# Moving the weight pieces and the small tiles of a decoder layer to the other end of the SBUF partition

## The chip, the core and the metric

The kernel runs on one core of one Trainium2 chip. The metric is device microseconds (us) of one execution, the median of several runs. Durations of single instructions are given in nanoseconds (ns).

## What is computed

One layer of a hybrid decoder on 256 tokens of width 2048, all in float32. The reference, cut to its skeleton:

```
h = rms_norm(x, pre_mix_g)
rq, rk, rv, rg, dq, dk, dv, su, sv = split(h @ w_in)          # 2048 -> 6400
y = concat(retention(rq, rk, rv, rg),                          # 6 heads x 128
           diff_attention(dq, dk, dv),                         # 6 heads x 128
           spatial_gating(su, sv))                             # 4 groups x 128
x = x + rms_norm(y @ w_out, post_mix_g)                        # 2048 -> 2048
h = rms_norm(x, pre_ffn_g)
f = (silu(h @ w_gate) * (h @ w_up)) @ w_down                   # 2048 -> 5632 -> 2048
out = x + rms_norm(f, post_ffn_g)
```

## The kernel before

All big products go through one helper, `matmul_chunk` (line 94). It takes a chunk of at most 512 output columns (384 for the heads of differential attention) and walks over the contraction dimension in blocks of 128 rows (a K-block). A weight piece is two K-blocks. `split_weights` (line 71) loads it into a tile `raw` by DMA, ScalarE rounds it to `hi` (line 75), and VectorE makes `lo = raw - hi` (line 77). `accumulate` (line 80) then issues three matmuls for each K-block and each of the two blocks of 128 tokens, because the activation is split the same way:

```
nc.tensor.matmul(ps, lhsT=a_hi, rhs=wh, start=first, stop=False)   # L83
nc.tensor.matmul(ps, lhsT=a_lo, rhs=wh, start=False, stop=False)   # L84
nc.tensor.matmul(ps, lhsT=a_hi, rhs=wl, start=False, stop=last)    # L85
```

The activation slice (`lhsT`, 128 x 128) is the stationary operand. It is loaded into the array by a weight load, which the profile shows as an engine of its own, PEld. The weight piece (`rhs`, 128 x 512) is the moving operand, streamed from SBUF. So every matmul of a projection reads two places of SBUF: an activation tile, and a weight piece. The transposes and small attention products are put between chunks by generators that `advance()` steps.

The stages, with the stationary activation of each: the input projection (6 retention heads, 6 differential heads, 2 pairs of gating groups) with `x_hi` and `x_lo`; the output projection with `y_hi` and `y_lo`; gate and up, 11 chunks each, with `x1_hi` and `x1_lo`, which take the place of `x_hi` and `x_lo` in the pool `act` (the profile calls both `x_hi`, `x_lo`); down, 4 chunks of 44 K-blocks, with `h_hi` and `h_lo`.

SBUF is given out by pools, in the order in which they are opened, each one behind the one before. `const` and `act` come first, then `wpool` (the weight pieces), `small` and `ft`, then what is opened and closed later: `ypool` (y), the attention tiles, the tiles `oz` of the output projection, and at last `hpool` (h), which takes the place of `ypool` and what followed it. The built program places the operands of the projections so (bytes from the partition's start; a K-block of an activation is 1024 bytes and a token block 512, so all slices of a tile have the tile's remainder by 512; a weight piece is 4096 bytes a slot and its K-blocks start at multiples of 512 from the tile, so this holds for them too):

| tile | role | start | remainder by 512 |
|---|---|---|---|
| x_hi (x1_hi) | stationary | 17760 | 352 |
| x_lo (x1_lo) | stationary | 34144 | 352 |
| hi, 5 slots | moving | 83296 | 352 |
| lo, 5 slots | moving | 103776 | 352 |
| y_hi | stationary | 129504 | 480 |
| y_lo | stationary | 145888 | 480 |
| h_hi | stationary | 129504 | 480 |
| h_lo | stationary | 174560 | 480 |

The pool `small` takes 1152 bytes, which is 2 x 512 + 128; that is where the 128 bytes between the two remainders come from.

Of the kernel before, what the change touches and what calls it, by code (L numbers as in the profile page):

```python
# [32 lines left out]
def trunk(  # L33
# [24 lines left out]

    const = ctx.enter_context(tc.tile_pool(name="const", bufs=1))
    act = ctx.enter_context(tc.tile_pool(name="act", bufs=1))  # L60
    wpool = ctx.enter_context(tc.tile_pool(name="wpool", bufs=5))
    small = ctx.enter_context(tc.tile_pool(name="small", bufs=2))
    ft = ctx.enter_context(tc.tile_pool(name="ft", bufs=2))
    ps_acc = ctx.enter_context(tc.tile_pool(name="ps_acc", bufs=4, space=bass.MemoryType.PSUM))
    ps_tr = ctx.enter_context(tc.tile_pool(name="ps_tr", bufs=2, space=bass.MemoryType.PSUM))
    ps_mx = ctx.enter_context(tc.tile_pool(name="ps_mx", bufs=2, space=bass.MemoryType.PSUM))
# [1 line left out]
    def acc_tile():  # L68
        return ps_acc.tile([P, 512], F32, tag="acc", name="acc")

    def split_weights(src, kbs, width):
        raw = wpool.tile([P, kbs, width], F32, tag="raw", name="raw", bufs=4)
        nc.sync.dma_start(out=raw, in_=src)
        hi = wpool.tile([P, kbs, width], F32R, tag="hi", name="hi")
        nc.scalar.copy(out=hi, in_=raw)  # L75
        lo = wpool.tile([P, kbs, width], F32R, tag="lo", name="lo")
        nc.vector.tensor_tensor(out=lo, in0=raw, in1=hi.bitcast(F32), op=ALU.subtract)  # L77
        return hi, lo

    def accumulate(ps, ah, al, wh, wl, kb, tb, first, last):  # L80
        a_hi = ah[:, kb, tb * P:(tb + 1) * P]
        a_lo = al[:, kb, tb * P:(tb + 1) * P]
# [3 lines that stand above are left out]
# [3 lines left out]
    def advance():  # L89
        for g in list(pending):  # L90
            if next(g, "end") == "end":
                pending.remove(g)

    def matmul_chunk(src, kbs, width, ah, al, lead=0, fine=0, on_tb=None, hooks=(), held=None):
        """accs[tb] = a[tb] @ w over kbs K-blocks; token block 0 runs `lead` subtiles ahead of block 1."""
        accs = [acc_tile() for _ in range(NT)]
        subs = []
        kb = 0
        while kb < kbs:
            n = 1 if kb < fine else 2  # L100
            subs.append((kb, n))
            kb += n
        held = held or {}
        for i in range(len(subs) + lead):
            for tb in range(NT):
                k = i - lead * tb
                if not 0 <= k < len(subs):
                    continue
                k0, n = subs[k]
                if k not in held:  # L110
                    piece = src[k0 // 2]
                    held[k] = split_weights(piece[:, k0 % 2:k0 % 2 + n], n, width)
                hi, lo = held[k]
                for j in range(n):
                    accumulate(accs[tb][:, :width], ah, al, hi[:, j], lo[:, j], k0 + j, tb,
                               k0 + j == 0, k0 + j == kbs - 1)
                if k == len(subs) - 1 and on_tb is not None:
                    on_tb(tb, accs[tb])
            if i < len(hooks) and hooks[i] is not None:
                hooks[i]()  # L120
            advance()
        return accs
# [6 lines left out]
        nc.gpsimd.tensor_scalar(out=ve, in0=sums, scalar1=scale, scalar2=eps, op0=ALU.mult, op1=ALU.add)  # L129
        nc.gpsimd.tensor_tensor(out=out_t, in0=ve, in1=neg_half[:, :n], op=ALU.pow)  # L130

# [1 line left out]
    neg_half = const.tile([P, 8], F32, tag="neg_half", name="neg_half")  # L133
    nc.gpsimd.memset(neg_half, -0.5)
    warm = const.tile([P, 8], F32, tag="warm", name="warm")
# [9 lines left out]
    x_lo = act.tile([P, KB, T], F32R, tag="a_lo", name="x_lo")  # L145
    x_sb = act.tile([P, NT, D], F32, tag="x", name="x_sb")

    # ================= token mixer =================
    with ExitStack() as mctx:
        ypool = mctx.enter_context(tc.tile_pool(name="ypool", bufs=1))  # L150
        y_hi = ypool.tile([P, KB, T], F32R, tag="y_hi", name="y_hi")
# [36 lines left out]
        def load_x(tb):  # L188
            nc.sync.dma_start(out=x_sb[:, tb], in_=x[tb * P:(tb + 1) * P])
            for c in range(4):  # L190
                sq = hd.tile([P, 512], F32, tag="sq1", name="sq1", bufs=1)
                nc.scalar.activation(out=sq, in_=x_sb[:, tb, c * 512:(c + 1) * 512], func=AF.Square,
                                     accum_out=ss_1[:, tb, c:c + 1])
# [171 lines left out]
        def sgu_pair(p, kb, accs):  # L365
# [46 lines left out]
            for g in range(2):  # L412
                put_y(kb + g, ys[g])

        first = {0: split_weights(w_ret[0, 0][:, 0:1], 1, 512)}
        load_xT(0, 1, hi_on_dve=True)
        load_order = [(1, 1, True), (2, 2), (4, 2), (6, 2), (8, 2), (10, 2), (12, 2), (14, 2)]
        hooks = [lambda a=a: load_xT(*a) for a in load_order]
        accs = matmul_chunk(w_ret[0], KB, 512, x_hi, x_lo, fine=2, hooks=hooks, held=first)
        pending.append(ret_head(0, 0, accs, wait=5))  # L420
        accs = matmul_chunk(w_ret[1], KB, 512, x_hi, x_lo,
                            hooks=[lambda: load_x(0), None, lambda: load_x(1), None, token_stats])
        small_loads()
        pending.append(ret_head(1, 1, accs))
        for h in range(2, NH):
            accs = matmul_chunk(w_ret[h], KB, 512, x_hi, x_lo)
            pending.append(ret_head(h, h, accs))
        for h in range(NH):
            accs = matmul_chunk(w_diff[h], KB, 384, x_hi, x_lo)
            pending.append(diff_head(h, NH + h, accs))  # L430
        load_sgu()
        for p in range(NG // 2):
            accs = matmul_chunk(w_sgu[p], KB, 512, x_hi, x_lo)
            pending.append(sgu_pair(p, 2 * NH + 2 * p, accs))

# [1 line left out]
        accs0 = matmul_chunk(w_out[0], KB, 512, y_hi, y_lo)  # L437
        while pending:
            advance()
# [71 lines left out]
            nc.gpsimd.tensor_scalar(out=hr2, in0=rstd2, scalar1=0.5, scalar2=None, op0=ALU.mult)  # L511
            nc.gpsimd.tensor_tensor(out=hrr, in0=hr2, in1=rstd2, op=ALU.mult)

# [1 line left out]
        def start_residual():  # L515
            pending.append(residual())

# [13 lines left out]

        up0 = matmul_chunk(w_up[0], KB, 512, x1_hi, x1_lo, hooks=[None] * 3 + [finish_gate0])

    # ================= feed forward =================
    hpool = ctx.enter_context(tc.tile_pool(name="hpool", bufs=1))
    h_hi = hpool.tile([P, HB, T], F32R, tag="h_hi", name="h_hi")
    h_lo = hpool.tile([P, HB, T], F32R, tag="h_lo", name="h_lo")
# [17 lines left out]
    for c in range(1, NCH):  # L555
        accs = matmul_chunk(w_gate[c], KB, 512, x1_hi, x1_lo)
        aa = [gate_part(tb, accs[tb]) for tb in range(NT)]
        accs = matmul_chunk(w_up[c], KB, 512, x1_hi, x1_lo)
# [124 lines left out]
```

## Time and profile before

| | |
|---|---|
| time, median of 3 runs | 1153.27 us (1153.09 to 1153.86) |
| span of the profiled execution | 1151.1 us |
| TensorE matmul (PE) busy | 1136.2 us, 99% |
| weight load (PEld) busy | 951.0 us, 83% |
| VectorE (DVE) busy | 636.5 us, 55% |
| ScalarE (ACT) busy | 530.1 us, 46% |
| DMA | 221.34 MB, mean 192 GB/s |
| granted TensorE clock | 0.998 |

The span runs from the first to the last instruction of the program; the profiled execution has no time of its own beside it. The timed runs are 2.0 to 2.8 us longer than this span, 2.2 us at the median. A matmul's recorded duration runs from its start to a modelled end, and the next one starts before that end; how fast TensorE goes is read from start to start.

### The profile page before, as it was taken

The numbers are of one execution on the slowest core, as the hardware profiler recorded it, in microseconds if no ns is written. First come the engines' busy times: TensorE is split into PE (matmuls) and PEld (weight loads), VectorE is DVE, ScalarE is ACT, GpSimd is POOL, SyncE is SP. The second block draws the span as 40 slices with busy tenths as digits, with TensorE's granted clock in tenths as the row PEclk, the third lists the DMA queues.
The fourth block names the chain that finished last, engine by engine and source line by source line (L and its number), as shares of the span: only waits on it lengthen the run. The fifth ranks groups of instructions, "written<-read, shape, count | busy, mean of one in ns | idle before, by whom it ended". The sixth has DMA issues, their size and how long they took to land.

```text
span 1151.1 us, 13889 instructions
## 1 busy us (share of the span) xinstructions
PE 1136.2 (99%) x5266; PEld 951.0 (83%) x5266; DVE 636.5 (55%) x759; ACT 530.1 (46%) x720; POOL 27.1 (2%) x56
## 2 busy tenths in 40 slices
PE   7999999999999999999999999999999999999997
PEld 6888899998878778888888888888888888888885
DVE  6655455656767595555555555554554544444444
ACT  7644445656634464444444444444444434343332
POOL 0000000000100000000000000000000000000000
PEclk9999999999999999999999999999999999999999
DMA  9755555565566447556555555555555655655553
GB/s 348 265 187 191 164 165 175 174 214 175 185 219 220 163 150 234 184 187 197 185 188 194 186 189 193 186 193 189 188 196 185 221 194 186 185 190 192 164 184 110
DMA packets 64468, 221.34 MB, mean 192 GB/s; under 512 B 7168, under 2 KB 9232, under 8 KB 63760
## 3 DMA queue, kind: packets, MB, share of 16 engines
q1 hardware_dynamic: 64368, 220.43, 58.3%
q8 instruction: 41, 0.67, 0.3%
q14 instruction: 27, 0.22, 0.1%
q0 software_dynamic: 32, 0.02, 0.0%
HBM read 218.32 MB, written 2.10 MB: 191 GB/s over the span
## 4 chain that ended last, share of the span: by engine, by line
PE 97%; DVE 1%; issue 1%; DMA 0%; ACT 0%; POOL 0%; DVEq 0%; POOLq 0%
PE acc L83 31%; PE acc L85 31%; PE acc L84 31%; PE h_ps L548 1%; PE qk_ps L220 0%; PE sc L252 0%; DMA cols<-in_cols_dram 0%; PE yt_ps L176 0%; DVE x_lo L479 0%; PE o_ps L229 0%; PE o_ps L228 0%; PE o_ps L227 0%; PE sc L329 0%; PE x_ps L476 0%; DVE fg L589 0%
## 5 line engine op out<-in xcount | busy, mean ns | idle before, releaser
L77 DVE TENSOR_TENSOR lo<-raw,hi 128x1024 fp32r<-128x1024 f32 (+2 forms) x409 | 486.1, 1190 | 462.8 <-ACT hi L75 441.2
L75 ACT CAST hi<-raw 128x1024 fp32r<-128x1024 f32 (+2 forms) x409 | 418.5, 1025 | 553.7 <-PE acc L84 496.2
L83 PE MATMUL acc<-hi,x_hi 128*128 128x512 f32 (+1 forms) x1152 | 444.0, 386 | 6.2 <-DVE x_hi L166 6.2
L84 PE MATMUL acc<-hi,x_lo 128*128 128x512 f32 (+1 forms) x1152 | 438.7, 381 | 0.0
L85 PE MATMUL acc<-lo,x_hi 128*128 128x512 f32 (+1 forms) x1152 | 438.6, 381 | 0.0
L83 PEld LDWEIGHTS acc<-hi,x_hi 128*128 128x128 f32 x1152 | 216.8, 188 | 44.2 <-issue 8.1
L85 PEld LDWEIGHTS acc<-lo,x_hi 128*128 128x128 f32 x1152 | 216.7, 188 | 37.9
L84 PEld LDWEIGHTS acc<-hi,x_lo 128*128 128x128 f32 x1152 | 216.9, 188 | 36.8 <-DVE x_lo L169 0.4
L83 PE MATMUL acc<-hi,h_hi 128*128 128x512 f32 x352 | 139.0, 395 | 0.0
L85 PE MATMUL acc<-lo,h_hi 128*128 128x512 f32 x352 | 138.9, 395 | 0.0
L84 PE MATMUL acc<-hi,h_lo 128*128 128x512 f32 x352 | 138.9, 395 | 0.0
L85 PEld LDWEIGHTS acc<-lo,h_hi 128*128 128x128 f32 x352 | 66.3, 188 | 15.6
L84 PEld LDWEIGHTS acc<-hi,h_lo 128*128 128x128 f32 x352 | 66.3, 188 | 15.4
L83 PEld LDWEIGHTS acc<-hi,h_hi 128*128 128x128 f32 x352 | 66.3, 188 | 15.3
L83 PE MATMUL acc<-hi,y_hi 128*128 128x512 f32 x128 | 50.9, 400 | 0.0
L84 PE MATMUL acc<-hi,y_lo 128*128 128x512 f32 x128 | 50.5, 396 | 0.0
L85 PE MATMUL acc<-lo,y_hi 128*128 128x512 f32 x128 | 50.4, 395 | 0.0
L83 PEld LDWEIGHTS acc<-hi,y_hi 128*128 128x128 f32 x128 | 24.0, 188 | 5.8 <-ACT y_hi L178 0.3
L85 PEld LDWEIGHTS acc<-lo,y_hi 128*128 128x128 f32 x128 | 24.1, 188 | 5.5
L84 PEld LDWEIGHTS acc<-hi,y_lo 128*128 128x128 f32 x128 | 24.1, 188 | 5.4
L585 POOL TENSOR_TENSOR ro_f<-ss_t,neg_half 128x1 f32<-128x1 f32 x2 | 1.1, 548 | 711.0 <-DVE ss_t L583 711.0
L520 ACT ACTIVATE fa<-acc,hr 128x512 f32<-128x512 f32 x22 | 15.0, 685 | 5.7 <-PE acc L85 5.3
(133 smaller groups left out, 423.7 us busy)
## 6 DMA issues: line engine op xcount, KB each, us to landing
raw<-in_w_gate_dram SPq DMA_DIRECT2D x88, 512.0 KB, 3.5
raw<-in_w_up_dram SPq DMA_DIRECT2D x88, 512.0 KB, 3.5
raw<-in_w_down_dram SPq DMA_DIRECT2D x88, 512.0 KB, 3.5
raw<-in_w_ret_dram SPq DMA_DIRECT2D x47, 512.0 KB, 4.5
raw<-in_w_diff_dram SPq DMA_DIRECT2D x48, 384.0 KB, 3.3
raw<-in_w_out_dram SPq DMA_DIRECT2D x32, 512.0 KB, 4.2
raw<-in_w_sgu_dram SPq DMA_DIRECT2D x16, 512.0 KB, 4.4
x_sb<-in_x_dram SPq DMA_DIRECT2D x2, 1024.0 KB, 8.1
```

The costliest lines, as they stand in the source:

```text
L75: nc.scalar.copy(out=hi, in_=raw)
L77: nc.vector.tensor_tensor(out=lo, in0=raw, in1=hi.bitcast(F32), op=ALU.subtract)
L83: nc.tensor.matmul(ps, lhsT=a_hi, rhs=wh, start=first, stop=False)
L84: nc.tensor.matmul(ps, lhsT=a_lo, rhs=wh, start=False, stop=False)
L85: nc.tensor.matmul(ps, lhsT=a_hi, rhs=wl, start=False, stop=last)
L520: nc.scalar.activation(out=a, in_=acc, func=AF.Tanh, scale=hr2[:, tb:tb + 1])
L548: nc.tensor.transpose(out=pt[:, i], in_=aa[tb][:, i * P:(i + 1) * P], identity=ident)
L585: nc.gpsimd.tensor_tensor(out=ro_f[:, tb:tb + 1], in0=ss_t[:, tb:tb + 1], in1=neg_half[:, :1], op=ALU.pow)
```

## The change

The three pools `wpool`, `small` and `ft` are opened on the right side, so they are given out from the far end of the partition downwards. What is opened behind them moves down into the space that they leave. Nothing else changes: the instructions of each engine, their order and the semaphores that they wait for are the same in both built programs, since the lifetimes of all tiles and the order of the pools on the left are the same. The diff, without comment lines that it drops:

```diff
-    wpool = ctx.enter_context(tc.tile_pool(name="wpool", bufs=5))
-    small = ctx.enter_context(tc.tile_pool(name="small", bufs=2))
-    ft = ctx.enter_context(tc.tile_pool(name="ft", bufs=2))
+    wpool = ctx.enter_context(tc.tile_pool(name="wpool", bufs=5, side="right"))
+    small = ctx.enter_context(tc.tile_pool(name="small", bufs=2, side="right"))
+    ft = ctx.enter_context(tc.tile_pool(name="ft", bufs=2, side="right"))
```

The operands of the projections then lie so:

| tile | start before | start after | remainder by 512, before | after |
|---|---|---|---|---|
| x_hi, x_lo | 17760, 34144 | the same | 352 | 352 |
| y_hi, y_lo | 129504, 145888 | 66912, 83296 | 480 | 352 |
| h_hi, h_lo | 129504, 174560 | 66912, 111968 | 480 | 352 |
| hi, lo | 83296, 103776 | 188384, 208864 | 352 | 480 |

Stationary less moving, by 512, is 0 in the x stages and 128 in the y and h stages before; it is 384 (the same as -128) in all stages after.

## Rows read from the trace of the kernel before

**Rows 1.** The page: span, busy time by engine, shares of the chain that ended last.

```profile
span 1151.1 us, 13889 instructions
PE 1136.2 (99%) x5266; PEld 951.0 (83%) x5266; DVE 636.5 (55%) x759; ACT 530.1 (46%) x720; POOL 27.1 (2%) x56
PE 97%; DVE 1%; issue 1%; DMA 0%; ACT 0%; POOL 0%; DVEq 0%; POOLq 0%
```

**Rows 2.** Busy time by engine in four stretches: stages x, y, gate/up, down.

```profile
core 0: us, PE busy (x) PEld busy (x) DVE busy (x) ACT busy (x) POOL busy (x), PEclk, DMA share, GB/s
25.00:50.00 25.00, 25.00 (x112) 20.72 (x111) 13.77 (x19) 16.91 (x31) 2.14 (x3) 1.00 0.87 312
...
345.00:385.00 40.00, 40.00 (x174) 32.41 (x173) 30.40 (x29) 18.46 (x26) 0.00 (x0) 1.00 0.65 211
465.00:501.00 36.00, 36.00 (x161) 29.81 (x160) 18.95 (x18) 15.25 (x16) 0.00 (x0) 1.00 0.59 192
1000.00:1041.00 41.00, 41.00 (x178) 33.26 (x177) 18.85 (x18) 16.96 (x19) 0.00 (x0) 1.00 0.59 184
```

**Rows 3.** Groups by line and shape, whole span; L84 of each stationary operand.

```profile
L84 PE MATMUL acc<-hi,x_lo 128*128 128x512 f32 x960 | 374.5, 390 | 0.0
...
L84 PEld LDWEIGHTS acc<-hi,x_lo 128*128 128x128 f32 x1152 | 216.9, 188 | 36.8 <-DVE x_lo L169 0.4
...
L84 PE MATMUL acc<-hi,h_lo 128*128 128x512 f32 x352 | 138.9, 395 | 0.0
L84 PEld LDWEIGHTS acc<-hi,h_lo 128*128 128x128 f32 x352 | 66.3, 188 | 15.4
...
L84 PE MATMUL acc<-hi,x_lo 128*128 128x384 f32 x192 | 64.2, 334 | 0.0
...
L84 PE MATMUL acc<-hi,y_lo 128*128 128x512 f32 x128 | 50.5, 396 | 0.0
```

**Rows 4.** Timeline, PE, gate/up: first and last of 161 matmuls in a row.

```profile
464.67 0.39 PE L85 MATMUL acc<-lo,x_hi 128*128 128x512 f32 x1
...
500.94 0.39 PE L83 MATMUL acc<-hi,x_hi 128*128 128x512 f32 x1
```

**Rows 5.** Timeline, PE, down: first and last of 178 matmuls in a row.

```profile
999.77 0.39 PE L85 MATMUL acc<-lo,h_hi 128*128 128x512 f32 x1
...
1040.90 0.39 PE L85 MATMUL acc<-lo,h_hi 128*128 128x512 f32 x1
```

**Rows 6.** Timeline, PE, output projection: first and last of 174 in a row.

```profile
344.79 0.40 PE L84 MATMUL acc<-hi,y_lo 128*128 128x512 f32 x1
...
384.98 0.40 PE L83 MATMUL acc<-hi,y_hi 128*128 128x512 f32 x1
```

**Rows 7.** Timeline, PE, differential heads: first and last of 45, 384 columns wide.

```profile
199.82 0.33 PE L83 MATMUL acc<-hi,x_hi 128*128 128x384 f32 x1
...
207.45 0.34 PE L85 MATMUL acc<-lo,x_hi 128*128 128x384 f32 x1
```

**Rows 8.** Timeline, PE, gate/up around the transposes between two chunks.

```profile
502.30 1.03 PE L548 MATMUL h_ps<-ident,fa 128*128 128x128 f32 x8
503.09 0.48 PE L83 MATMUL acc<-hi,x_hi 128*128 128x512 f32 x1
503.41 0.39 PE L84 MATMUL acc<-hi,x_lo 128*128 128x512 f32 x1
...
504.79 0.39 PE L84 MATMUL acc<-hi,x_lo 128*128 128x512 f32 x1
...
506.83 0.39 PE L84 MATMUL acc<-hi,x_lo 128*128 128x512 f32 x1
```

## The prediction

> **What bounds the kernel now.** The page comes first: TensorE is busy 99% of the span, and the chain that ended last is 97% TensorE [rows 1]. DVE and ACT have 45% and more of the span to spare, so a change pays or costs only where it alters the pace of the matmuls. [...] No wait is there to be removed. What is left is the spacing of the matmuls while nobody waits, and there the stages differ, which is the finding this forecast rests on.
>
> The groups by shape hint at it: the same line with the same 128x512 shape has a mean of 390 ns with x as stationary, 395 ns with h and 396 ns with y [rows 3]. These durations have a modelled end, so I took start to start from the timeline. Gate/up: 161 starts, (500.94 - 464.67) / 160 = 226.7 ns [rows 4]. Down: 178 starts, (1040.90 - 999.77) / 177 = 232.4 ns [rows 5]. Output projection: 174 starts, (384.98 - 344.79) / 173 = 232.3 ns [rows 6]. So y and h run 5.7 ns a matmul behind x, at the same clock, shape and moving tiles. Differential heads, 384 columns, stationary x: 45 starts, 7.63 / 44 = 173.4 ns [rows 7]. The 128 columns between 384 and 512 cost 53.3 ns, 0.416 ns a column, so 512 columns need 213.3 ns; x pays 13.4 ns on top at either width, y and h pay 19.0. It is a price per weight load, not per column.
>
> What differs between x and y or h is only where the stationary tile lies: higher up in the partition, and with a remainder by 512 bytes that is 128 larger. The moving tiles are the same for all.
>
> Two rows narrow it down. The weight load takes 188 ns for x and for h alike [rows 3]; the loading does not get longer, the matmul that runs over it does. And h covers 90 KB of the partition, y only the lowest 32 KB of that stretch, yet both run at the same 232.3 to 232.4 ns; a price that grew with distance would show. I therefore read it as two streams of reads, the weight load's and the matmul's, that get in each other's way or not depending on how their addresses stand to each other: 0 by 512 is good, 128 is bad.
>
> After a break x is slow for a moment as well: behind the transposes six spacings take (504.79 - 503.41) / 6 = 230 ns, then nine take (506.83 - 504.79) / 9 = 226.7 [rows 8]. So x finds into the faster rhythm within about six matmuls; the y and h stretches of 173 and 177 spacings do not find it.
>
> **The change, part by part.** No instruction, order or wait changes, and with TensorE as the bound [rows 1] the other engines' accesses at new addresses have 45% of slack to hide any difference; I cost them at nothing. What uncovers this is only a VectorE group that grew by more than that 45%, for which no row speaks. The small tiles and `ft` are read by ACT, DVE and the 11 sets of transposes (88 of them); nothing there either. Three edits remain.
>
> y and h move down to x's remainder, 352. There are 128 x 3 matmuls with y and 352 x 3 with h, on three lines each [rows 3]: 1440. If they reach x's spacing they give 1440 x 5.68 = 8.2 us. Some 12 breaks in these stages (the last gating steps, eight sets of transposes of the second norm, the last h) keep up to six slow ones each, 0.4 us, so 7.8 us. The other bound is nothing.
>
> The moving tiles go from 352 to 480. No row shows a moving weight piece at this remainder, so I bound it by the two spacings that exist: 226.7 and 232.4. For the 960 x 3 = 2880 matmuls of 512 columns with x or x1 the loss is between nothing and 2880 x 5.68 = 16.4 us; up to six behind each of about 40 breaks (four TensorE steps in each retention head, 11 sets of transposes, some of the rest) are slow already, 1.2 us, so 15.2 us. The 192 x 3 = 576 matmuls of 384 columns lie between nothing and 3.3 us; as the price goes by the weight load and not by the column, 3.0 us less breaks.
>
> Which value holds depends on the difference of the two addresses, and that is 384 by 512 in every stage after the change: neither the good 0 nor the bad 128. If the pattern repeats every 256 bytes, 384 is 128 and all stages are slow. If it repeats every 512, 384 is a case of its own, and of the two differences seen one is good and one bad. Nothing in these rows can choose between 256 and 512. I take the slow value: one half for sure and part of the other half.
>
> The sum: y and h stay as they are, 0; x at 512 columns +15.2; x at 384 columns +3.0; in all +18.2 us. Against the profiled span, 1151.1 + 18.2 = 1169.3 us; with the 2.2 us by which the median of the timed runs lies above that span, 1171.5 us.
>
> [...] The trace shows one matmul shape at 226.7 and 232.4 ns with nothing changed but the place of its stationary tile [rows 4, 5]. [...]
>
> **Rivals.**
>
> *The stationary tile's own place decides* (faster). Then the remainder 352 is good in itself, or the lower part of the partition is, and the moving tile's place is indifferent. For it: x, the good case, keeps its place, and y and h get exactly its remainder and come down next to it. Against it: the weight load is no longer in the bad case than in the good one [rows 3], so a place that is bad in itself should show there. It also covers a pattern of 512 bytes in which 384 happens to be good. Time: 1153.3 - 7.8 = 1145.5 us. It decides as soon as the x stages keep 226.7 ns; if then only part of h gains (the upper half of h_lo, say, in a matter of height), the time lies between 1145.5 and 1151.
>
> *Nothing changes* (same). Either placement has no effect and the 5.7 ns come from something else that goes with the stage, or the border between good and bad lies between the end of x_lo (50528) and the new start of y and h (66912), so that y and h stay bad and x good. [...] Against it: the two slow stages have different widths of weights in flight, different evacuations and different neighbours, and share with each other only the place. Time: 1153.3 us.
>
> *All stages slow, but worse than 232.4.* A new difference may be worse than the known bad one. No row prices it; the range's top leaves a little room only.
>
> **How the numbers follow.** Two streams in each other's way at 384: 0.48, time 1171.5, its own range 1167 to 1173.5 (without the breaks' allowance and with all 384-wide matmuls, 16.4 + 3.3 = 19.7 gives 1173.0; without the 384-wide ones at all, 15.2 gives 1168.5). Stationary place alone, or 384 good: 0.40, time 1145.5, its own range 1144.8 to 1151. Nothing changes: 0.10. Worse than known: 0.02. The two big cases have opposite signs and nearly the same chance, so the range must reach over both: 1144.8 to 1173.5. Faster by over 0.2% (2.3 us, about what a measurement of this kernel can tell from no change): 0.40; within it 0.10; slower 0.48 + 0.02 = 0.50.
>
> **What the changed profile would show.** Read start to start in the same five places. Right: gate/up and the input projection at about 232 ns, the 384-wide heads near 179, output projection and down still at 232, weight loads still 188 ns, granted clock 1.00, and DVE and ACT busy times within 1% of before. The first rival: gate/up at 226.7 and also y and h at 226.7. The second: all five as before. What would make the prediction wrong in its base rather than its sign: a spacing that is neither 226.7 nor 232.4, DVE or ACT instructions that change their durations with the place, or an idle gap of TensorE that was not there.

## The result, and the profile after

The change makes the kernel slower: 1169.15 us (1168.86 to 1170.53, 4 runs) against 1153.18 us beside it, a ratio of 1.0142 with a 95% interval of 1.013 to 1.0154. The forecast was 1171.5 us within 1144.8 to 1173.5. Of the executions behind the times below, one of the ten of experiment 3 took 1575.26 us at a granted clock of 0.68 and is left out of its ratio; all others were granted 0.99 or more.

The page first: span, busy time by engine, and the shares of the chain that ended last.

```profile
span 1167.3 us, 13889 instructions
PE 1152.5 (99%) x5266; PEld 954.0 (82%) x5266; DVE 637.0 (55%) x759; ACT 529.0 (45%) x720; POOL 26.9 (2%) x56
PE 98%; issue 1%; DMA 0%; DVE 0%; ACT 0%; DVEq 0%; POOL 0%; POOLq 0%
```

The same counts of instructions as in [rows 1], TensorE busy for 16.3 us more, the span 16.2 us longer, the weight loads (PEld) 3.0 us more, and VectorE, ScalarE and GpSimd within 1.1 us of before. No new wait: the time went into TensorE's own busy time. The stretches by window (PE, PEld, DVE, ACT, POOL; clock, DMA share, GB/s), which answer to [rows 2], say the same: no gap, and a granted clock of 1.00.

```profile
350.00:390.00 40.00, 40.00 (x174) 32.43 (x173) 30.14 (x28) 18.42 (x26) 0.00 (x0) 1.00 0.64 209
472.00:508.00 36.00, 36.00 (x157) 29.18 (x156) 18.38 (x18) 14.92 (x15) 0.00 (x0) 1.00 0.58 185
1000.00:1041.00 41.00, 41.00 (x178) 33.26 (x177) 19.13 (x17) 16.94 (x19) 0.00 (x0) 1.00 0.57 188
```

Gate/up has 157 matmuls in 36 us where it had 161; the output projection and down have the same 174 and 178 as before. Start to start in the timeline, first and last row of each stretch (157, 174, 178 and 47 matmuls in a row):

```profile
471.61 0.39 PE L84 MATMUL acc<-hi,x_lo 128*128 128x512 f32 x1
...
507.86 0.39 PE L84 MATMUL acc<-hi,x_lo 128*128 128x512 f32 x1
...
349.64 0.39 PE L85 MATMUL acc<-lo,y_hi 128*128 128x512 f32 x1
...
389.84 0.40 PE L84 MATMUL acc<-hi,y_lo 128*128 128x512 f32 x1
...
999.73 0.39 PE L84 MATMUL acc<-hi,h_lo 128*128 128x512 f32 x1
...
1040.86 0.39 PE L84 MATMUL acc<-hi,h_lo 128*128 128x512 f32 x1
...
202.63 0.34 PE L84 MATMUL acc<-hi,x_lo 128*128 128x384 f32 x1
...
210.72 0.34 PE L85 MATMUL acc<-lo,x_hi 128*128 128x384 f32 x1
```

| stretch | before | after |
|---|---|---|
| gate/up, stationary x1 | 226.7 ns [rows 4] | 36.25 / 156 = 232.4 ns |
| output projection, y | 232.3 ns [rows 6] | 40.20 / 173 = 232.4 ns |
| down, h | 232.4 ns [rows 5] | 41.13 / 177 = 232.4 ns |
| differential heads, x, 384 columns | 173.4 ns [rows 7] | 8.09 / 46 = 175.9 ns |

All stages of 512 columns now have one spacing, the slow one. The mean weight load is as long as it was within 1 ns [rows 3], here for the stationary x and h:

```profile
L84 PEld LDWEIGHTS acc<-hi,x_lo 128*128 128x128 f32 x1152 | 217.5, 189 | 41.1 <-DVE x_lo L169 0.4
...
L84 PEld LDWEIGHTS acc<-hi,h_lo 128*128 128x128 f32 x352 | 66.3, 188 | 15.4
```

The mean hides something. The shortest, median and longest load of one line in gate/up, before and after:

```profile
L84 PEld LDWEIGHTS acc<-hi,x_lo x54: 187/188/188, 464.9 to 500.9; 128*128 128x128 f32 x54
...
L84 PEld LDWEIGHTS acc<-hi,x_lo x52: 187/188/192, 472.1 to 507.6; 128*128 128x128 f32 x52
```

In the fast stretch no load is longer than 188 ns; in the slow one some take 192. In the down stage of the kernel before, slow as well, one load in seven does (152 of 1056), and it is the load that runs in the longest spacing of each seven, 240 or 241 ns. So the loads of a slow stage show it too, by 4 ns in every seventh.

And behind the transposes between two chunks x no longer finds into a faster rhythm, as it did in [rows 8]: thirteen spacings take (513.16 - 510.14) / 13 = 232.3 ns.

```profile
509.03 1.04 PE L548 MATMUL h_ps<-ident,fa 128*128 128x128 f32 x8
509.82 0.48 PE L83 MATMUL acc<-hi,x_hi 128*128 128x512 f32 x1
510.14 0.39 PE L84 MATMUL acc<-hi,x_lo 128*128 128x512 f32 x1
...
513.16 0.39 PE L85 MATMUL acc<-lo,x_hi 128*128 128x512 f32 x1
```

Where the 16.2 us arise is read from landmarks of the program in both timelines and chains. Before:

```profile
149.01 0.33 PE L83 MATMUL acc<-hi,x_hi 128*128 128x384 f32 x1
263.64 0.39 PE L83 MATMUL acc<-hi,x_hi 128*128 128x512 f32 x1
458.05 0.87 PE h_ps L548 x8
902.39 0.87 PE h_ps L548 x8
```

After:

```profile
151.67 0.35 PE L83 MATMUL acc<-hi,x_hi 128*128 128x384 f32 x1
267.57 0.39 PE L83 MATMUL acc<-hi,x_hi 128*128 128x512 f32 x1
463.70 0.87 PE h_ps L548 x8
918.62 0.87 PE h_ps L548 x8
```

The differential heads start 2.7 us later and end 3.9 us later; the first set of transposes of the feed forward comes 5.65 us later, the eleventh 16.23 us; the rest, down with h alone, adds nothing. So the stages of 384 columns cost 1.3 us, the x and x1 stages of 512 columns 16.2 - 1.3 = 14.9 us, y and h nothing.

### The profile page after: what moved, and what is told of

It reads as the page before. It is cut to its first block, busy times and chain, and to the rows that moved or that the text cites. A ratio compares the mean times of both kernels' runs of the same rounds, so it can differ in the third digit from the quotient of the medians.

```text
span 1167.3 us, 13889 instructions
## 1 busy us (share of the span) xinstructions
PE 1152.5 (99%) x5266; PEld 954.0 (82%) x5266; DVE 637.0 (55%) x759; ACT 529.0 (45%) x720; POOL 26.9 (2%) x56
## 4 chain that ended last, share of the span: by engine, by line
PE 98%; issue 1%; DMA 0%; DVE 0%; ACT 0%; DVEq 0%; POOL 0%; POOLq 0%
PE acc L83 32%; PE acc L85 31%; PE acc L84 31%; PE h_ps L548 1%; PE qk_ps L220 0%; PE sc L252 0%; DMA cols<-in_cols_dram 0%; PE x_ps L476 0%; PE yt_ps L176 0%; PE o_ps L229 0%; PE o_ps L228 0%; PE o_ps L227 0%; PE sc L329 0%; DVE fg L589 0%; PE pm L406 0%
## 5 line engine op out<-in xcount | busy, mean ns | idle before, releaser
L83 PE MATMUL acc<-hi,x_hi 128*128 128x512 f32 (+1 forms) x1152 | 449.4, 390 | 6.1 <-DVE x_hi L166 6.1
L84 PE MATMUL acc<-hi,x_lo 128*128 128x512 f32 (+1 forms) x1152 | 444.3, 386 | 0.0
L85 PE MATMUL acc<-lo,x_hi 128*128 128x512 f32 (+1 forms) x1152 | 444.0, 386 | 0.0
L83 PEld LDWEIGHTS acc<-hi,x_hi 128*128 128x128 f32 x1152 | 217.4, 189 | 48.6 <-issue 8.1
L85 PEld LDWEIGHTS acc<-lo,x_hi 128*128 128x128 f32 x1152 | 217.3, 189 | 42.3
L84 PEld LDWEIGHTS acc<-hi,x_lo 128*128 128x128 f32 x1152 | 217.5, 189 | 41.1 <-DVE x_lo L169 0.4
L83 PE MATMUL acc<-hi,h_hi 128*128 128x512 f32 x352 | 139.0, 395 | 0.0
L85 PE MATMUL acc<-lo,h_hi 128*128 128x512 f32 x352 | 138.9, 395 | 0.0
L84 PE MATMUL acc<-hi,h_lo 128*128 128x512 f32 x352 | 138.9, 395 | 0.0
L83 PEld LDWEIGHTS acc<-hi,h_hi 128*128 128x128 f32 x352 | 66.3, 188 | 15.5
L84 PEld LDWEIGHTS acc<-hi,h_lo 128*128 128x128 f32 x352 | 66.3, 188 | 15.4
L85 PEld LDWEIGHTS acc<-lo,h_hi 128*128 128x128 f32 x352 | 66.3, 188 | 15.4
L83 PE MATMUL acc<-hi,y_hi 128*128 128x512 f32 x128 | 50.9, 400 | 0.0
L84 PE MATMUL acc<-hi,y_lo 128*128 128x512 f32 x128 | 50.5, 396 | 0.0
L85 PE MATMUL acc<-lo,y_hi 128*128 128x512 f32 x128 | 50.4, 395 | 0.0
L83 PEld LDWEIGHTS acc<-hi,y_hi 128*128 128x128 f32 x128 | 24.0, 188 | 5.8 <-ACT y_hi L178 0.3
L85 PEld LDWEIGHTS acc<-lo,y_hi 128*128 128x128 f32 x128 | 24.1, 188 | 5.5
L84 PEld LDWEIGHTS acc<-hi,y_lo 128*128 128x128 f32 x128 | 24.1, 188 | 5.4
```

## The experiments

The theory: the difference of the two addresses that TensorE reads at a time, the stationary tile that is being loaded and the moving tile that streams, sets the spacing. (In gate/up of the kernel before, the load for L84 starts at 464.90 us and takes 0.19 us; the matmul of L83 starts at 464.90 us as well, and that of L84 at 465.12 us.) The rivals: the place of the stationary tile, the place of the moving tile (each by its height or by its own remainder). Unused bytes move tiles without changing any instruction.

**1. y and h alone moved by 384 bytes, in the kernel before.**

```diff
     ft = ctx.enter_context(tc.tile_pool(name="ft", bufs=2))
+    gap = ctx.enter_context(tc.tile_pool(name="gap", bufs=1))
+    gap.tile([P, 96], F32, tag="gap", name="gap")
```

> The kernel before with 384 unused bytes behind the pool ft: y and h stay in the upper part of the partition but get the remainder 352 by 512, so stationary less moving is 0 in every stage. If the difference of the two addresses decides: y and h run at 226.7 ns like x, 1145.5 us (ratio to before 0.993). If the height in the partition decides (low is good): nothing changes, 1153 us.

Measured: 1144.96 us, ratio to before 0.993 (0.9916 to 0.9945). Down, first and last of 182 matmuls in a row (the two lines more shift L83 to L85):

```profile
999.80 0.39 PE L85 MATMUL acc<-hi,h_hi 128*128 128x512 f32 x1
...
1040.83 0.39 PE L86 MATMUL acc<-hi,h_lo 128*128 128x512 f32 x1
```

41.03 / 181 = 226.7 ns. y and h lie as high as before, 384 bytes higher in fact, and run like x. Height is out; so is the time of the stage, its width or its neighbours.

**2. The changed kernel with its weight pieces moved by 128 bytes.**

```diff
+    gap = ctx.enter_context(tc.tile_pool(name="gap", bufs=1, side="right"))
+    gap.tile([P, 32], F32, tag="gap", name="gap")
     wpool = ctx.enter_context(tc.tile_pool(name="wpool", bufs=5, side="right"))
```

> The changed kernel with 128 unused bytes at the far end, so the weight pieces lie at the far end with remainder 352 and stationary less moving is 0 everywhere. If the difference decides: all stages at 226.7 ns, 1145.5 us, the same as the kernel before with the unused bytes, and 24 us faster than the changed kernel. If weight pieces at the far end are slow by their place: all stages at 232.4 ns, 1169 us.

Measured: 1145.04 us, ratio 0.993 (0.9914 to 0.9947). With the whole change in place and 128 bytes more, the kernel is 24 us faster than the changed one. The far end is not slow. Gate/up, first and last of 125:

```profile
471.72 0.39 PE L87 MATMUL acc<-lo,x_hi 128*128 128x512 f32 x1
...
499.82 0.39 PE L85 MATMUL acc<-hi,x_hi 128*128 128x512 f32 x1
```

28.10 / 124 = 226.6 ns, where the changed kernel has 232.4.

**3. Everything moved by 128 bytes, in the kernel before.**

```diff
+    gap = ctx.enter_context(tc.tile_pool(name="gap", bufs=1))
+    gap.tile([P, 32], F32, tag="gap", name="gap")
     const = ctx.enter_context(tc.tile_pool(name="const", bufs=1))
```

> The kernel before with 128 unused bytes ahead of every pool: all operands move up by 128 bytes, so every remainder changes (x and weights 480, y and h 96) and no difference does. If the difference decides: as before, x at 226.7 and y and h at 232.4 ns, 1153 us. If the stationary tile's own remainder decides (480 is bad): x goes to 232.4 ns, 1168 us or more; if the moving tile's own remainder decides (480 is bad): all stages at 232.4 ns, 1169 us.

Measured: 1152.78 us, ratio 0.9999 (0.999 to 1.0009), its span 1151.0 us as before. x and the weight pieces now have the remainder 480, which y and h had in the slow case, and x stays at 226.6 ns; y and h have 96, a new one, and stay slow:

```profile
471.83 0.39 PE L86 MATMUL acc<-hi,x_lo 128*128 128x512 f32 x1
...
499.93 0.39 PE L87 MATMUL acc<-lo,x_hi 128*128 128x512 f32 x1
...
999.67 0.39 PE L87 MATMUL acc<-lo,h_hi 128*128 128x512 f32 x1
...
1040.80 0.39 PE L87 MATMUL acc<-lo,h_hi 128*128 128x512 f32 x1
```

(125 and 178 matmuls: 28.10 / 124 = 226.6 and 41.13 / 177 = 232.4 ns.) No tile's own remainder decides. These three leave the difference.

**4. A ladder of differences.** The weight piece of each chunk of gate and up is written a given number of bytes into a wider slot:

```diff
...
+    def piece_tile(kbs, width, tag):
+        t = wpool.tile([P, 1152], F32R, tag=tag, name=tag, bufs=4)
+        o = shift[0] // 4
+        return t[:, o:o + kbs * width].rearrange("p (k w) -> p k w", k=kbs)
...
-        hi = wpool.tile([P, kbs, width], F32R, tag="hi", name="hi")
+        hi = piece_tile(kbs, width, "hi")
...
-        lo = wpool.tile([P, kbs, width], F32R, tag="lo", name="lo")
+        lo = piece_tile(kbs, width, "lo")
...
+        shift[0] = SHIFTS[2 * c]
         accs = matmul_chunk(w_gate[c], KB, 512, x1_hi, x1_lo)
...
```

> A ladder: the kernel before with four slots for hi and lo instead of five, 512 bytes wider each, and in each of the 22 chunks of gate and up the weight piece written that many bytes into its slot: 0, 16, 32 and so on to 192, then in steps of 32 to 288, then 320 to 480. Stationary less moving is minus that many bytes. If the pattern repeats every 256 bytes: 226.7 ns at 0 and 256, 232.4 at 128 and 384, and the second half of the ladder repeats the first. If it repeats every 512 and 384 is bad by itself: the two halves differ. If only whole 128-byte blocks count, the spacing changes at the steps where a block's border is passed and not in between. No other effect on the time than through these spacings is expected; the total lies between 1150 and 1165 us.

**5. The ladder again with fine steps.** Only the list of bytes differs from the first ladder.

> The ladder again with fine steps around the two good places: the 22 chunks of gate and up are written 0, 4, 8, 12, 20, 24, 28, 240, 244, 248, 252, 256, 260, 264, 268, 272, 508, 504, 500, 496, 192 and 0 bytes into their slots. If the pattern repeats every 256 bytes down to its detail: 4 and 260 alike, 8 and 264, 252 and 508, 248 and 504, each pair within 0.3 ns. If the good case is one exact place: only 0 and 256 at 226.7 ns. If it is a window: its neighbours within a few bytes on one or both sides are at 226.7 too.

Measured in both, from the timeline: mean start to start in the later 70 or so matmuls of each chunk, without spacings across a missing record, in ns; another choice of stretch moves a value by about 0.1. The row 0 is the last chunk of the fine ladder, since the first chunk of both lies among breaks. The left column is moving less stationary, by 256; the column "upper" holds the same plus 256. In this count the change puts every stage at 128, and y and h before it stand at 384.

| by 256 | in the lower 256 | in the upper 256 |
|---|---|---|
| 0 | 226.7 | 226.7 |
| 4 | 236.7 | 236.5 |
| 8 | 233.3 | 233.3 |
| 12 | 228.9 | 228.9 |
| 16 | 231.7 | 231.7 |
| 28 | 226.8 | - |
| 32 | 233.2 | 233.3 |
| 64 | 229.0 | 229.0 |
| 96 | 233.4 | 233.3 |
| 128 | 232.4 | 233.3 |
| 160 | 234.1 | 234.3 |
| 192 | 233.3 | 233.3 |
| 224 | 233.3 | 233.3 |
| 240 | 236.7 | 236.7 |
| 244 | 239.8 | 239.9 |
| 248 | 230.0 | 233.3 |
| 252 | 226.7 | 226.7 |

Not in the table: 20 gives 236.0 and 24, 48, 144 and 176 give 233.3; 80 and 112 give 231.1. Two chunks of the fine ladder, at 4 (82 matmuls) and at 256 bytes (92), by first and last row:

```profile
437.81 0.40 PE L92 MATMUL acc<-hi,x_lo 128*128 128x512 f32 x1
...
456.98 0.40 PE L92 MATMUL acc<-hi,x_lo 128*128 128x512 f32 x1
...
663.32 0.39 PE L91 MATMUL acc<-hi,x_hi 128*128 128x512 f32 x1
...
683.95 0.39 PE L92 MATMUL acc<-hi,x_lo 128*128 128x512 f32 x1
```

19.17 / 81 = 236.7 and 20.63 / 91 = 226.7 ns. The pattern repeats every 256 bytes: of 16 pairs 14 agree within 0.3 ns, 128 and 384 are 0.9 ns apart and 248 and 504 are 3.3 apart. A difference can have more than one rhythm: y and h of the kernel before run at 232.4 ns with the difference at which the ladder has 233.3. That settles what the prediction left open: within 1 ns the change's 384 is the known bad 128. The good case is neither one place nor a window: 0, 252 and 28 have it, 4 bytes beside 0 costs 10 ns, and whole 128-byte blocks do not count, since the spacing moves within 4 bytes. The ladders' times were 1168.85 and 1169.53 us (one run each); the first lies above the 1150 to 1165 expected, and the spacings alone do not explain it. By the timeline its span exceeds that of the kernel before by 16.1 us: 11.3 us are the spacings in gate and up (a mean of 232.2 against 226.8 ns), 3.4 us are longer breaks there, nearly all in the first chunk, and 1.2 us arise in down, with ten short breaks that the kernel before lacks. So the expectation that nothing else would act on the time was wrong. TensorE now waits, for the transposes' input and for a weight piece:

```profile
PE x_ps L484 <- DVE hx L480: 1.7, 1, 1.7
PE acc L93 <- DVE lo L85: 1.1, 1, 1.1
```

The ladders have four slots for hi and lo where the kernel before has five, a likely cause that no run tests by itself. The means in the table leave the breaks out.

**6. All operands at multiples of 512.** The kernel of experiment 1 with 160 unused bytes ahead of every pool:

```diff
+    low = ctx.enter_context(tc.tile_pool(name="low", bufs=1))
+    low.tile([P, 40], F32, tag="low", name="low")
     const = ctx.enter_context(tc.tile_pool(name="const", bufs=1))
```

> The first padded kernel (difference 0 in every stage) with 160 more unused bytes ahead of every pool, so that all operands of the projections start at a multiple of 512 bytes. If only the difference counts: the same as that kernel, 226.7 ns in every stage, 1145 us. If the 13.4 ns that even the good case pays on top of its 512 columns come from tiles that start inside a 128-byte block: down to some 213 to 216 ns a matmul, 512 columns alone at the rate of the rows, about 1085 us.

Measured: 1145.48 us, ratio 0.9937 (0.9922 to 0.9952). Down, first and last of 182:

```profile
999.75 0.39 PE L89 MATMUL acc<-lo,h_hi 128*128 128x512 f32 x1
...
1040.78 0.39 PE L87 MATMUL acc<-hi,h_hi 128*128 128x512 f32 x1
```

41.03 / 181 = 226.7 ns again. The 13.4 ns that remain in the good case, by the prediction's estimate from [rows 4, 7], do not come from where tiles start within 512 bytes.

**7. y and h alone put right, in the changed kernel.**

```diff
     ft = ctx.enter_context(tc.tile_pool(name="ft", bufs=2, side="right"))
+    gap = ctx.enter_context(tc.tile_pool(name="gap", bufs=1))
...
     x_sb = act.tile([P, NT, D], F32, tag="x", name="x_sb")
+    gap.tile([P, 32], F32, tag="gap", name="gap")
```

> The changed kernel with 128 unused bytes between x and y: y and h stay low and the weight pieces at the far end, but y and h get the weight pieces' remainder, so their difference is 0 while that of x stays at 384. If the differences act by stage and add up: y and h at 226.7 ns, x at 232.4, the changed kernel's 1169 us less 7.8 us, 1161 us. If what x does disturbs the later stages or the height decides: 1169 us.

Measured: 1161.47 us, ratio to before 1.0077 (1.006 to 1.0094). Gate/up (122 matmuls) and down (183):

```profile
471.65 0.39 PE L84 MATMUL acc<-hi,x_hi 128*128 128x512 f32 x1
...
499.77 0.40 PE L85 MATMUL acc<-hi,x_lo 128*128 128x512 f32 x1
...
999.73 0.39 PE L84 MATMUL acc<-hi,h_hi 128*128 128x512 f32 x1
...
1040.99 0.39 PE L86 MATMUL acc<-lo,h_hi 128*128 128x512 f32 x1
```

28.12 / 121 = 232.4 and 41.26 / 182 = 226.7 ns: the stages are independent and add up, 1169.15 - 7.8 = 1161.35 expected.

**8. Only x_lo at difference 128.** In the kernel before:

```diff
+    act.tile([P, 32], F32, tag="gap1", name="gap1")
     x_lo = act.tile([P, KB, T], F32R, tag="a_lo", name="x_lo")
     x_sb = act.tile([P, NT, D], F32, tag="x", name="x_sb")
+    act.tile([P, 96], F32, tag="gap2", name="gap2")
```

> The kernel before with 128 unused bytes between x_hi and x_lo (and 384 more behind x, so that the weight pieces, y and h keep their remainders): of the three matmuls of a K-block in the x stages only L84's stationary tile lies at difference 128, the other two at 0. L84's weight load runs while the matmul of L83 streams. If the load that runs meanwhile is what gets in the matmul's way: the spacing behind L83 grows and the other two stay near 226.7 ns. If a matmul is slow because of its own stationary tile: the spacing behind L84 grows instead. If any bad load throws the rhythm of all: all three near 232 ns. Time: 1/3 of the whole loss to all of it, 1158 to 1169 us.

Measured: 1165.13 us (one run), inside the range but with none of the three pictures. Three K-blocks in a row from the timeline:

```profile
480.19 0.40 PE L83 MATMUL acc<-hi,x_hi 128*128 128x512 f32 x1
480.42 0.40 PE L84 MATMUL acc<-hi,x_lo 128*128 128x512 f32 x1
480.65 0.39 PE L85 MATMUL acc<-lo,x_hi 128*128 128x512 f32 x1
480.88 0.40 PE L83 MATMUL acc<-hi,x_hi 128*128 128x512 f32 x1
...
482.27 0.40 PE L83 MATMUL acc<-hi,x_hi 128*128 128x512 f32 x1
```

Nine spacings take 2.08 us, 231.1 ns each; over all of gate/up the mean is 232.5 behind L83, 234.1 behind L84 and 226.9 behind L85. The spacing behind the matmul over which the bad load runs (L83) grows, and so does the one behind the next (L84); the third is near the fast value. So my picture that only the matmul streaming meanwhile pays was too simple. The weight loads in gate/up, 465 to 501 us, do not point at the bad tile either (shortest, median, longest):

```profile
L84 PEld LDWEIGHTS acc<-hi,x_lo x53: 187/188/188, 464.9 to 501.0; 128*128 128x128 f32 x53
...
L85 PEld LDWEIGHTS acc<-lo,x_hi x52: 192/192/193, 465.2 to 500.5; 128*128 128x128 f32 x52
```

The load of x_lo, at the bad difference, takes its 188 ns; the one after it, of x_hi at difference 0, takes 192 every time. Whether the second stretch comes from the slow matmul's own tile or is the first one's disturbance carried over stays open.

## Why the prediction was right

*What bounds the kernel.* Right: TensorE stays the bound, busy for 99% of the span, with no gap and a granted clock of 1.00 in the three windows, and the busy times of VectorE and ScalarE stay within 0.2%.

*The difference of the addresses, not the place.* Right, and shown: experiments 1 and 2 put the difference right at either end of the partition and get 226.7 ns everywhere, and experiment 3 moves every place and leaves every difference and gets no change of time. The mechanism behind it, two streams of reads in each other's way, was only argued; the runs show the dependence on the difference, not the collisions. The step "the loading does not get longer" rested on a mean: in the slow stretches of 512 columns about every seventh load takes 192 instead of 188 ns.

*384 is like 128.* The prediction took the slow value, half because a pattern of 256 bytes would force it. It could not choose between 256 and 512 from its rows; the ladder did. So the sign was in good part luck: slower had 0.50 and faster 0.40, and the range had to reach over both.

*y and h stay as they are, 0.* Right: 232.4 ns in both stages.

*x at 512 columns, +15.2 us.* Measured 14.9. (At the 5.68 ns and six matmuls a break that gave 0.4 us for 12 breaks, 40 breaks come to 1.4 us and not 1.2, and the term to 15.0.)

*x at 384 columns, +3.0 us.* The term that was mis-sized: measured 1.3 us. I had read "a price per weight load, not per column" off the good case and carried it to the bad one. The bad case costs 175.9 - 173.4 = 2.5 ns at 384 columns in the stretch shown, 5.7 at 512. That is most of the 2.0 us between the sum's 18.2 and the 16.2 measured on the span. The other 0.35 us between 1171.5 and 1169.15 lie in the term that led from span to time: 2.2 us in the sum, 1.85 after the change.

*The rivals.* The first, the stationary tile's own place, would have given 1145.5 us; the changed kernel is not that, but the time it names is what a difference of 0 gives: experiments 1 and 2. The second, no effect of placement, is refuted by every run but the third. Its "different widths of weights in flight" was no argument against it: both slow stages have pieces of 512 columns [rows 3]. In experiment 2, moving the weight pieces by 128 bytes takes 24 us off the changed kernel.

*The best version.* The kernel before with 384 unused bytes behind `ft`, 1144.96 us (0.993, 0.9916 to 0.9945), beats both kernels, and the change with 128 bytes more (experiment 2, 1145.04 us) is as fast: in both the difference is 0 in every stage, and the stretches read run at 226.7 and 226.6 ns.

## What to carry to other kernels

When TensorE is busy all the time, read the spacing of its matmuls start to start, stage by stage: here stages of one shape stood at 226.7 and 232.4 ns, a cost that no wait showed. Where the moving and the stationary operand are float32r tiles as here, allocate them so that their starts differ by a multiple of 256 bytes, which gave 226.7 ns at 0 and at 256 in the ladders, where the other differences gave 226.7 to 239.9 (here all slices within a tile begin at multiples of 512 bytes from its start, so the tiles' starts decide); a pad of 384 bytes did it in experiment 1, 1144.96 us, and one of 128 bytes in experiment 2, 1145.04 us. A new small tile that is given out between the two can undo it: 128 bytes ahead of x_lo alone gave 1165.13 us in experiment 8; the same 128 bytes ahead of both did nothing in experiment 3, 1152.78 us. An edit that only moved tiles was not free of effect here, 16 us: work out the differences of the addresses before and after, for every pair that is read together.

## What was not expected of the hardware

The spacing depends on the difference in a fine and rugged way, from 226.7 to 239.9 ns: 4 bytes beside the best place costs 10.0 ns, 4 bytes on its other side nothing. The slow stages are not noisy but periodic, though casts and DMA run beside them (in down VectorE is busy for 18.85 of 41 us and ScalarE for 16.96, at a DMA share of 0.59 [rows 2]): before the change the spacings in down repeat after seven, 1627 ns for the seven (232.4 each) along the stage but for its breaks, and gate/up of the changed kernel has the same 1627 ns. No difference of the 40 tried (by 512) went below 226.7 ns, 13.4 above the 213.3 that 512 columns cost by the prediction's estimate from the rows; where these come from is open, except that it is not the start of the tiles within 512 bytes.
